# Convolution stage: the first GLU block ahead of q, its output written by parity, four weight sums in other tiles

## The chip, the cores and the metric

The kernel runs on one core of a Trainium2 chip. The metric is device time in microseconds (us): the median of the runs shown. A profiled execution gives, for every engine, when each instruction started and how long it took.

## What is computed

The reference is one layer of a streaming encoder on a sequence of 2048 tokens of 1024 channels, in fp32:

```python
h = rms_norm(x, norm_g) * (1.0 + scale) + shift          # scale, shift, gate: from silu(c) @ w_ada
u = h @ w_in                                             # 1024 -> 5632 columns
glu_in, gate_a, q, k, v, gate_b, m_a, m_b = split(u)
a, b = split(glu_in);  g = a * sigmoid(b)                # GLU, 512 channels
y_a = conv31_depthwise_causal(g) -> layer_norm -> silu, * silu(gate_a) -> @ w_conv_out
y_b = (stick_breaking_attention(rms(q), rms(k), v) * silu(gate_b)) @ w_sb_out
y = sigmoid(m_a) * y_a + sigmoid(m_b) * y_b
x = x + gate * (y @ w_out)
```

## The kernel before

Every fp32 operand of a large product is split into a rounded part `hi` and a rest `lo` (fp32r), and three matmuls (`mm3`, L135) make one product. Channels lie on the 128 partitions, tokens in four chunks of 512. The planner of the framework orders each engine's instructions by priority and by the times it expects; on each engine, and on SyncE's queue (SP) that issues the DMAs, they then run in that order. `tc.keep_in_program_order` pins some of them to program order; `pin[0]` switches this on for all matmuls, transposes and convolution taps that follow.

**Norm stage (L452 to L618).** The chunks are normed in the order of `ORDER` (3, 2, 1, 0) into the tiles `hT(g)`. The first chunk's q, k and v blocks are made here; the weights of the first q group, `w2_q0`, lie in the two pairs `whi`/`wlo` of pool `wpa` and stay there. The last chunk is normed from pool `hz` (L616): `xt` tiles are loaded, scaled, transposed by TensorE (`pt`), and `hf` minus `hhi` gives `hlo` on GpSimd (POOL) and VectorE (DVE).

**Convolution stage (L625 to L763), pool `cvp`.** It works through a fixed list of blocks (L740 to L760): q group 0 on the three later chunks, GLU 0, a SiLU gate, GLU 1, q group 1, a gate, GLU 2, k group 2, v group 4, GLU 3, k group 3, then four SiLU gates. A GLU block (`glu`, L693) is eight tiles of 24 matmuls of 512 columns: four tiles of b, whose sigmoid ScalarE (ACT) writes into `u` (L705), and four of a, which DVE multiplies into `u` (L713). `u` holds even and odd tokens in two rows. A q or k group (`qk_group`, L312) has two half tiles of 48 matmuls of 256 columns a chunk; some steps later `head_norm` (DVE) and transposes (TensorE) follow. A SiLU gate (`silu_block`, L718) has four tiles; each goes through one buffer `sg`: sigmoid on ACT, product on DVE (L726), DMA out, and only then the next sigmoid.

**Taps.** The depthwise convolution of a GLU block (`conv`, L636) is 51 DVE instructions in the list `todo`: `pre` (tile `v`), 47 taps (L661, L664) into tiles `ca`, `cc`, `cb`, and three that combine them. After each tile `tick` takes RATE of them on average from the list; what is left at the stage's end is issued there.

**Weights.** A piece (`piece`, `split_into` L98) is two halves of 512 columns: DMA into `wl` (two buffers in all), cast on ACT to `whi` (L102), rest on POOL to `wlo` (L103). The pairs rotate: two in `wpa`, one in `wpb`. Between pieces `prepare` (L220) makes two of 28 sums of blocks of w_out (for a fast product at the end of the kernel): one or two loads into `wl`, an add on POOL (L234), a cast (L237), a rest (L238), and two DMAs to DRAM (`ws_d`). A sum's rounded half goes to one tile, its rest to the other, and both lie in the rotating pairs.

After the stage come LayerNorm with the last v group and gates (L767 on), the attention with the remaining gates (L918 on), and the output products.

Of the kernel before, what the change touches and what calls it, by code (L numbers as in the profile page):

```python
# [8 lines left out]
F32 = mybir.dt.float32  # L9
F32R = mybir.dt.float32r  # L10
BF16 = mybir.dt.bfloat16
I32 = mybir.dt.int32
AF = mybir.ActivationFunctionType
ALU = mybir.AluOpType
# [4 lines left out]
P = 128  # L19
SEQ = 2048  # L20
D = 1024
KC = D // P
CH = 512
# [8 lines left out]
MAGIC = 0x5F3759DF  # L32
NXT = 6
NWA = 4
RATE = 2.9
NEARLY = 3
HT = SEQ // 2
UW = HT + CW // 2 + 1
# [3 lines left out]
B_GLU_A, B_GLU_B, B_GA = 0, 4, 8  # L42
# [3 lines left out]
def f(ap):  # L46
    return ap.bitcast(F32)
# [3 lines left out]
def trunk_kernel(  # L51
# [20 lines left out]
    nc = tc.nc  # L72
# [4 lines left out]
    def dram(name, shape, dt):  # L77
        return dp.tile(shape, dt, name=name, tag=name)
# [33 lines left out]
    pin = [False]  # L112
# [50 lines left out]
    ws_d = {}  # L163
    o_d = [[dram(f"o{j}_{g}", [P, CH], F32) for g in range(NCH)] for j in range(JC)]

    wpa = ctx.enter_context(tc.tile_pool(name="wpa", bufs=2))
# [8 lines left out]
    def hT(g):  # L175
# [7 lines left out]
    SEVEN = {  # L183
# [7 lines left out]
    }  # L191
    LASTS = {(1, 0): 4, (1, 1): 3, (0, 0): 5, (0, 1): 5}
    H = KC // 2
# [7 lines left out]
    ORDER = list(reversed(range(NCH)))  # L201
    for g in ORDER[:3]:
        h_tiles(hp, g)
    with ExitStack() as s1:
# [9 lines left out]
        def piece(src):  # L214
            npiece[0] += 1
            return load_piece(wpb if npiece[0] % 3 == 0 else wpa, src)

        wanted = [(m, j) for m in SEVEN for j in range(H)]

        def prepare():  # L220

            npiece[0] += 1
            pool = wpb if npiece[0] % 3 == 0 else wpa
            hi = pool.tile([P, 1024], F32R, tag="whi", name="whi")
            lo = pool.tile([P, 1024], F32R, tag="wlo", name="wlo")
            for i in range(2):
                m, j = wanted.pop(0)
                s = slice(i * CH, (i + 1) * CH)
                w = []
                for r, c_, _ in SEVEN[m][0]:  # L230
                    w.append(wpa.tile([P, CH], F32, tag="wl", name="wl", bufs=2))
                    nc.sync.dma_start(w[-1], w_out[j + H * r][:, c_ * CH:(c_ + 1) * CH])
                if len(w) == 2:
                    nc.gpsimd.tensor_tensor(  # L234
                        out=w[0], in0=w[0], in1=w[1],
                        op=ALU.add if SEVEN[m][0][1][2] > 0 else ALU.subtract)
                nc.scalar.copy(out=hi[:, s], in_=w[0])  # L237
                nc.gpsimd.tensor_tensor(out=lo[:, s], in0=w[0], in1=f(hi[:, s]),  # L238
                                        op=ALU.subtract)
                ws_d[m, j] = dram(f"ws{m}_{j}", [P, 2, CH], F32)  # L240
                nc.sync.dma_start(ws_d[m, j][:, 0, :], f(hi[:, s]))
                nc.sync.dma_start(ws_d[m, j][:, 1, :], f(lo[:, s]))


        def nat_mm(ps, w2, b, half, i, kc, start, stop, part=(0, 2, 1)):
# [49 lines left out]
        def tick():  # L295
# [3 lines left out]
            for d in [d for d in deferred if d[0] <= 0]:  # L299
                deferred.remove(d)  # L300
                d[1]()
            credit[0] = min(credit[0] + RATE, 3 * RATE)
            n = int(credit[0])
# [8 lines left out]
        def qk_group(grp, isk, chunks, w2=None):  # L312

            w2 = w2 or [piece(w_qkv[grp, i]) for i in range(2)]
            h4 = (grp % 2) * 4
            dst = kst_d if isk else qst_d
            for b in chunks:
                ssq = sm.tile([P, 4, 4], F32, tag="ssq", name="ssq")
                qn = qp.tile([P, 4, 4, HD], F32, tag="qn", name="qn", bufs=2)
                pss = []  # L320
                for half in range(2):
                    ps = nat_tile(pd, w2, b, half)
                    pss.append(ps)
                    for i in range(2):
                        for h in range(4):
                            sq = qp.tile([P, HD], F32, tag="sqq", name="sqq", bufs=2)
                            nc.scalar.activation(
                                out=sq, in_=ps[:, i, h * HD:(h + 1) * HD], func=AF.Square,
                                accum_out=ssq[:, 2 * half + i, h:h + 1])
                    tick()  # L330
                later(1, lambda pss=pss, ssq=ssq, qn=qn: head_norm(pss, ssq, qn))
                for pr in range(2):
                    later(3 + pr, lambda qn=qn, b=b, pr=pr: transposed(qn, pr, dst, h4, b, isk))
# [118 lines left out]
        with tc.tile_pool(name="hx", reuse_waits="tile", bufs=1) as hx:  # L452
# [33 lines left out]
            def rest(w, p):  # L486
                for i in range(2):
# [4 lines left out]
            w2_q0 = [[wpa.tile([P, D], F32R, tag=t, name=t) for t in ("whi", "wlo")]  # L492
                     for _ in range(2)]
# [6 lines left out]
            ca = hx.tile([P, D], F32, name="ca", bufs=1)  # L500
# [5 lines left out]
            for i in range(2):  # L506
                s = slice(i * CH, (i + 1) * CH)
                ps = pt.tile([P, CH], F32, tag="pt", name="pc")
# [32 lines left out]
            for kc in range(KC):  # L541
                col = slice(kc, kc + 1)
                if kc == 0:
# [4 lines left out]
                               func=AF.Identity, scale=ng[:, col], bias=ba1[:, col])  # L548
# [3 lines left out]
                hi, lo = (h[kc] for h in hT(g0))  # L552
# [72 lines left out]
        with tc.tile_pool(name="cvp", reuse_waits="tile", bufs=2, side="right") as cvp:  # L625
            ca = cvp.tile([P, D], F32, tag="cc", name="ca", bufs=1)
# [66 lines left out]
            def glu(j):  # L693
                u = cvp.tile([P, 2, UW], F32, tag="u", name="u", bufs=2)
                nc.gpsimd.memset(u[:, :, HT:], 0.0)

                def at_(g):
                    return u[:, :, g * CH // 2:(g + 1) * CH // 2].rearrange("p t m -> p m t")

                w = piece(w_in[B_GLU_B + j])  # L700
                prepare()
                for g in ORDER:
                    ps = pd.tile([P, CH], F32, tag="pd", name="pd")
                    dense(ps, w, hT(g), KC)
                    nc.scalar.activation(out=at_(g), in_=ps.rearrange("p (m t) -> p m t", t=2),  # L705
                                         func=AF.Sigmoid)
                    tick()
                w = piece(w_in[B_GLU_A + j])
                prepare()
                for g in ORDER:  # L710
                    ps = pd.tile([P, CH], F32, tag="pd", name="pd")
                    dense(ps, w, hT(g), KC)
                    nc.vector.tensor_tensor(out=at_(g), in0=ps.rearrange("p (m t) -> p m t", t=2),  # L713
                                            in1=at_(g), op=ALU.mult)
                    tick()
                conv(j, u)

            def silu_block(blk, dst, after=None):  # L718
                w = piece(w_in[blk])
                prepare()  # L720
                for g in range(NCH):
                    ps = pd.tile([P, CH], F32, tag="pd", name="pd")
                    dense(ps, w, hT(g), KC)
                    sg = cvp.tile([P, CH], F32, tag="sg", name="sg", bufs=1)
                    nc.scalar.activation(out=sg, in_=ps, func=AF.Sigmoid)
                    nc.vector.tensor_tensor(out=sg, in0=ps, in1=sg, op=ALU.mult)  # L726
                    nc.sync.dma_start(dst[g], sg)
                    tick()
# [8 lines left out]
                                half)  # L737
                        tick()

            qk_group(0, False, ORDER[1:], w2_q0)  # L740
            pin[0] = True
            for kc in range(KC):
                todo.append(lambda kc=kc: mod_col(
                    16 + kc, ca, qp.tile([P, D], F32, tag="qn", name="wa", bufs=2)))
            todo.append(lambda: nc.vector.tensor_tensor(
                out=gate, in0=mod[:, 16:24], in1=ba[:, 16:24], op=ALU.add))
            glu(0)
            silu_block(B_GA, ga_d[0])
            glu(1)
            qk_group(1, False, ORDER[1:])  # L750
# [168 lines left out]
    with ExitStack() as s2:  # L919
# [206 lines left out]
        def operands(m, ch):  # L1126

            q = "zo"[turn[0] % 2]
            turn[0] += 1
            A, B = [], []  # L1130
            for j in range(H):
                A.append(operand(q, "a", j))
                nc.sync.dma_start(f(A[j]), ws_d[m, j])
            for kc in range(H):
                B.append(operand(q, "b", kc))
                t = combined(SEVEN[m][1], lambda t: y[ch + t[1], kc + H * t[0]],
                             lambda: yp.tile([P, CH], F32, tag="io", name="sum", bufs=8),
                             nc.gpsimd)
                nc.scalar.copy(out=B[kc][:, 0, :], in_=t)
                nc.vector.tensor_tensor(out=B[kc][:, 1, :], in0=t, in1=f(B[kc][:, 0, :]),  # L1140
                                        op=ALU.subtract)
            return A, B
# [45 lines left out]
        for n_, u in enumerate(units + [None]):  # L1188
            r = [None] * 4
            p = prev[0] if prev else None  # L1190
# [67 lines left out]
    with s3:  # L1258
# [12 lines left out]
        for ch in (0, 2):  # L1271
# [6 lines left out]
            for i, m in enumerate(order):  # L1278
                A, B = nxt
# [54 lines left out]
```

## Time and profile before

| | |
|---|---|
| median of 3 runs | 1886.64 us (1884.7 to 1890.9) |
| the profiled execution | 1885.76 us, of which 1883.9 us are the span of the instructions |
| TensorE (PE) busy | 1779.0 us, 94% |
| DVE / ACT / POOL busy | 1319.4 us, 70% / 836.2 us, 44% / 815.5 us, 43% |
| mean granted TensorE clock | 0.986 |
| HBM traffic | 139 GB/s over the span |

PE's busy share counts matmuls from start to modelled end, so a busy PE is not PE at its peak; its idle time is what is read here. "Idle before" in a row is the time an engine stood still ahead of that instruction, with the instruction or transfer that ended the wait. [...]

### The profile page before, as it was taken

What the parts mean: (1) busy time and instruction counts of PE and PEld (TensorE: products, weight loads), DVE (VectorE), ACT (ScalarE), POOL (GpSimd) and SP (SyncE); (2) the same over time, 40 slices, a digit from 0 to 9 for tenths busy, and PEclk for the clock granted to TensorE, in tenths of its full rate; (3) what the DMA queues carried; (4) which work ended last, traced back from release to release, by engine and by line L of the source; (5) the groups of instructions that cost most, each with busy time, mean ns of one, the idle gap of its engine ahead of it and who ended that gap; (6) DMA issues with size and microseconds to landing.
All of it is one profiled execution on the core that took longest, in us unless ns stands there. A gap on an engine that the chain in (4) does not pass through costs nothing.

```text
span 1883.9 us, 27529 instructions
## 1 busy us (share of the span) xinstructions
PE 1779.0 (94%) x9516; PEld 1503.8 (80%) x9516; DVE 1319.4 (70%) x1769; ACT 836.2 (44%) x1916; POOL 815.5 (43%) x987
## 2 busy tenths in 40 slices
PE   6899999999999699899999999999999989999998
PEld 5798889898898587778877787877878767887887
DVE  7645598798888654448777777777777787576475
ACT  5464223232232122237767776777777762121021
POOL 0343342331414333356666666666666662321050
PEclk9999999999999899999999999999999989999999
DMA  8553733516245543342322222222223257388365
GB/s 287 168 185 107 240 117 94 192 35 196 100 133 171 173 142 136 131 168 65 99 70 93 71 82 82 93 79 84 90 80 93 68 186 246 135 301 290 135 213 167
DMA packets 138335, 263.53 MB, mean 140 GB/s; under 512 B 17746, under 2 KB 30034, under 8 KB 138196
## 3 DMA queue, kind: packets, MB, share of 16 engines
q1 hardware_dynamic: 137044, 259.68, 41.7%
q10 hardware_dynamic: 1152, 2.10, 0.3%
q8 instruction: 75, 1.23, 0.3%
q14 instruction: 64, 0.52, 0.1%
HBM read 175.73 MB, written 85.98 MB: 139 GB/s over the span
## 4 chain that ended last, share of the span: by engine, by line
PE 54%; DVE 14%; DMA 10%; POOL 8%; issue 7%; ACT 5%; SPq 2%; DVEq 0%; ACTq 0%; POOLq 0%
PE pd L115 24%; PE p L115 8%; PE po L115 7%; PE av L115 5%; PE pT L120 5%; PE z L115 5%; POOL w L999 3%; DVE sc L992 2%; POOL wlo L103 2%; DVE cc L664 2%; DMA wl<-in_w_out_dram 1%; DVE ca L664 1%; DVE cb L664 1%; DVE tlo L1026 1%; DMA wl<-in_w_qkv_dram 1%
## 5 line engine op out<-in xcount | busy, mean ns | idle before, releaser
L999 POOL TENSOR_TENSOR w<-w,sc 128x512 f32<-128x512 f32 (+1 forms) x320 | 362.6, 1134 | 256.0 <-DVE sc L992 182.3
L115 PE MATMUL pd<-hhi,whi 128*128 128x512 f32 x1024 | 412.9, 403 | 1.0 <-ACT vsg L905 1.0
L115 PE MATMUL pd<-hhi,wlo 128*128 128x512 f32 x1024 | 402.4, 393 | 0.7 <-POOL wlo L103 0.7
L115 PE MATMUL pd<-hlo,whi 128*128 128x512 f32 x1024 | 402.0, 393 | 0.0
L992 DVE TENSOR_TENSOR_SCAN sc<-z,sc,w 128x512 f32<-128x512 f32 x192 | 245.0, 1280 | 91.3 <-ACT z L988 83.7
L987 ACT ACTIVATE w<-z 128x512 f32<-128x512 f32 (+1 forms) x320 | 172.2, 538 | 129.5 <-PE z L115 104.6
L115 PEld LDWEIGHTS pd<-hhi,wlo 128*128 128x128 f32 x1024 | 193.1, 189 | 43.7 <-POOL wlo L103 1.7
L115 PEld LDWEIGHTS pd<-hhi,whi 128*128 128x128 f32 x1024 | 195.2, 191 | 35.3 <-ACT vsg L905 1.4
L115 PEld LDWEIGHTS pd<-hlo,whi 128*128 128x128 f32 x1024 | 194.0, 189 | 34.3
L1026 DVE TENSOR_TENSOR tlo<-pT,thi 128x512 fp32r<-128x512 f32 (+1 forms) x320 | 184.4, 598 | 36.5 <-ACT thi L1025 33.6
L103 POOL TENSOR_TENSOR wlo<-wl,whi 128x512 fp32r<-128x512 f32 x88 | 137.4, 1572 | 150.5 <-ACT whi L102 138.4
L115 PE MATMUL z<-kt,q 128*128 128x512 f32 (+2 forms) x640 | 193.9, 384 | 8.9 <-DVE sc L992 8.0
L1025 ACT CAST thi<-pT 128x512 fp32r<-128x512 f32 (+1 forms) x320 | 165.3, 527 | 63.0 <-PE pT L120 59.4
L115 PE MATMUL pd<-whi,hhi 128*128 128x256 f32 x608 | 171.5, 290 | 17.7 <-DVE sg L726 15.8
L120 PE MATMUL pT<-ident,w 128*128 128x128 f32 x1088 | 173.5, 275 | 8.9 <-POOL w L999 8.6
L120 PEld LDWEIGHTS pT<-ident,w 128*128 128x128 f32 x1088 | 137.9, 141 | 44.8 <-POOL w L999 13.5
L988 ACT ACTIVATE z<-z 128x512 f32<-128x512 f32 (+1 forms) x320 | 171.7, 537 | 0.0
L115 PE MATMUL pd<-whi,hlo 128*128 128x256 f32 x608 | 168.7, 287 | 1.6 <-DVE hlo L131 1.0
L115 PE MATMUL pd<-wlo,hhi 128*128 128x256 f32 x608 | 156.1, 287 | 3.4 <-POOL wlo L103 3.4
L996 DVE TENSOR_TENSOR_SCAN sc<-z,tri 128x512 f32<-128x512 f32 (+3 forms) x128 | 104.4, 820 | 52.9 <-ACT z L988 42.4
L115 PE MATMUL av<-tlo,vt 128*128 128x512 f32 (+1 forms) x320 | 123.1, 385 | 14.7 <-DVE tlo L1026 11.2
L115 PEld LDWEIGHTS pd<-whi,hhi 128*128 128x128 f32 x608 | 118.9, 196 | 18.5 <-DVE sg L726 16.2
(296 smaller groups left out, 3186.2 us busy)
## 6 DMA issues: line engine op xcount, KB each, us to landing
wl<-in_w_in_dram SPq DMA_DIRECT2D x64, 256.0 KB, 3.0
za<-ws SPq DMA_DIRECT2D x28, 512.0 KB, 4.6
oa<-ws SPq DMA_DIRECT2D x28, 512.0 KB, 4.8
wa<-in_w_ada_dram SPq DMA_DIRECT2D x24, 512.0 KB, 5.4
wl<-in_w_out_dram SPq DMA_DIRECT2D x48, 256.0 KB, 2.9
wl<-in_w_qkv_dram SPq DMA_DIRECT2D x36, 256.0 KB, 2.7
xt<-in_x_n_dram SPq DMA_DIRECT2D x16, 512.0 KB, 5.3
vst<-st SPq DMA_DIRECT2D x64, 128.0 KB, 1.9
```

The source lines that it names most:

```text
L103: (lo_eng or nc.gpsimd).tensor_tensor(out=lo[:, s], in0=wl, in1=f(hi[:, s]), op=ALU.subtract)
L115: i = nc.tensor.matmul(*a, **k)
L120: i = nc.tensor.transpose(*a)
L664: keep(nc.vector.scalar_tensor_tensor(out=acc[f_], in0=x, scalar=tap_w(f_, a), in1=acc[f_], op0=ALU.mult, op1=ALU.add))
L987: nc.scalar.activation(out=w[:, lo:], in_=z[:, lo:], func=AF.Sigmoid, scale=HD ** -0.5)
L988: nc.scalar.activation(out=z[:, lo:], in_=z[:, lo:], func=AF.Sigmoid, scale=-HD ** -0.5)
L992: nc.vector.tensor_tensor_scan(out=s[:, 1:], data0=z, data1=w, initial=s[:, 0:1], op0=ALU.mult, op1=ALU.bypass)
L996: nc.vector.tensor_tensor_scan(out=s[:, lo + 1:], data0=z[:, lo:], data1=tri[:, :CH - lo], initial=1.0, op0=ALU.mult, op1=ALU.max)
L999: nc.gpsimd.tensor_tensor(out=w[:, lo:], in0=w[:, lo:], in1=s[:, lo:CH], op=ALU.mult)
L1025: nc.scalar.copy(out=thi[:, :n], in_=pT[:, :n])
L1026: nc.vector.tensor_tensor(out=tlo[:, :n], in0=pT[:, :n], in1=f(thi[:, :n]), op=ALU.subtract)
```

## The change

RATE goes from 2.9 to 2.75. `glu(0)` is traced ahead of the first q group, and the switch `pin[0] = True` moves behind it. The q group no longer uses the weights that lie in `wpa` but loads them again. In the first GLU block the weights of a are loaded right behind those of b. `prepare` makes one sum in one tile (rounded half left, rest right) and writes it with one DMA; the four sums of the first GLU block are made in the tiles `v` and `ca` of the convolution, the others, two at a time, in a pair as before. The two GLU instructions read PSUM with a step of two elements and write each row of `u` as one contiguous piece; before, they read PSUM in order and wrote alternately to the two rows.

```diff
-RATE = 2.9
+RATE = 2.75
...
-        def prepare():
+        def prepare(t):
+            m, j = wanted.pop(0)
+            w = []
+            for r, c_, _ in SEVEN[m][0]:
+                w.append(wpa.tile([P, CH], F32, tag="wl", name="wl", bufs=2))
+                nc.sync.dma_start(w[-1], w_out[j + H * r][:, c_ * CH:(c_ + 1) * CH])
+            if len(w) == 2:
+                nc.gpsimd.tensor_tensor(
+                    out=w[0], in0=w[0], in1=w[1],
+                    op=ALU.add if SEVEN[m][0][1][2] > 0 else ALU.subtract)
+            nc.scalar.copy(out=t[:, :CH], in_=w[0])
+            nc.gpsimd.tensor_tensor(out=t[:, CH:D], in0=w[0], in1=f(t[:, :CH]),
+                                    op=ALU.subtract)
+            ws_d[m, j] = dram(f"ws{m}_{j}", [P, D], F32)
+            nc.sync.dma_start(ws_d[m, j], f(t[:, :D]))
+        def prepare_two(early=False):
+            if early:
+                for tag, n in (("v", UW), ("ca", HT + 1)):
+                    prepare(cvp.tile([P, n], F32R, tag=tag, name=tag, bufs=1))
+                return
             npiece[0] += 1
             pool = wpb if npiece[0] % 3 == 0 else wpa
...
+            for t in [pool.tile([P, D], F32R, tag=t, name=t) for t in ("whi", "wlo")]:
+                prepare(t)
...
                 def at_(g):
-                    return u[:, :, g * CH // 2:(g + 1) * CH // 2].rearrange("p t m -> p m t")
+                    return u[:, :, g * CH // 2:(g + 1) * CH // 2]
+                def by_parity(ps):
+                    return ps.rearrange("p (m t) -> p t m", t=2)
                 w = piece(w_in[B_GLU_B + j])
-                prepare()
+                wa_ = piece(w_in[B_GLU_A + j]) if j == 0 else None
+                prepare_two(j == 0)
...
-                    nc.scalar.activation(out=at_(g), in_=ps.rearrange("p (m t) -> p m t", t=2),
-                                         func=AF.Sigmoid)
+                    nc.scalar.activation(out=at_(g), in_=by_parity(ps), func=AF.Sigmoid)
...
-                w = piece(w_in[B_GLU_A + j])
-                prepare()
+                w = wa_ or piece(w_in[B_GLU_A + j])
+                prepare_two(j == 0)
...
-                    nc.vector.tensor_tensor(out=at_(g), in0=ps.rearrange("p (m t) -> p m t", t=2),
-                                            in1=at_(g), op=ALU.mult)
+                    nc.vector.tensor_tensor(out=at_(g), in0=by_parity(ps), in1=at_(g),
+                                            op=ALU.mult)
...
-            qk_group(0, False, ORDER[1:], w2_q0)
-            pin[0] = True
             for kc in range(KC):
                 todo.append(lambda kc=kc: mod_col(
                     16 + kc, ca, qp.tile([P, D], F32, tag="qn", name="wa", bufs=2)))
             todo.append(lambda: nc.vector.tensor_tensor(
                 out=gate, in0=mod[:, 16:24], in1=ba[:, 16:24], op=ALU.add))
             glu(0)
+            pin[0] = True
+            qk_group(0, False, ORDER[1:])
             silu_block(B_GA, ga_d[0])
```

## Rows read from the trace of the kernel before

**Rows 1.** Stretches: length, busy us of PE, PEld, DVE, ACT, POOL, PEclk, DMA.

```profile
125.00:168.00 43.00, 40.66 (x332) 39.53 (x332) 23.42 (x58) 26.54 (x120) 14.19 (x13) 1.00 0.34 105
168.00:213.80 45.80, 45.08 (x207) 36.67 (x205) 16.14 (x29) 11.76 (x20) 14.72 (x13) 1.00 0.73 239
213.80:420.00 206.20, 203.28 (x1181) 180.16 (x1182) 178.94 (x183) 56.53 (x233) 70.20 (x44) 1.00 0.37 121
420.00:440.00 20.00, 15.17 (x108) 14.45 (x107) 15.32 (x34) 4.85 (x21) 5.90 (x4) 0.83 0.55 179
440.00:632.00 192.00, 192.00 (x1091) 168.91 (x1089) 165.12 (x167) 46.65 (x153) 57.05 (x34) 1.00 0.45 140
632.00:655.00 23.00, 7.24 (x49) 7.19 (x49) 10.89 (x10) 5.28 (x9) 10.40 (x8) 0.70 0.62 212
```

**Rows 2.** PE's waits from 100 to 700 us: total, times, longest.

```profile
PE pd L115 <- DVE sg L726: 15.8, 1, 15.8
PE pt L120 <- DVE qn L342: 4.4, 1, 4.4
```

**Rows 3.** Timelines (start, length) and SP's waits around the first GLU block's weights.

```profile
115.84 0.88 SPq L101 DMA_DIRECT2D wl<-in_w_in_dram  x2
...
131.17 1.84 SPq L403 DMA_DIRECT2D xt<-in_x_n_dram  x4
...
165.01 1.14 ACT L102 CAST whi<-wl 128x512 fp32r<-128x512 f32 x2 [2.46 <-PE pd L115]
...
SPq L627 <- PE pt L120: 18.7, 1, 18.7
...
147.92 7.97 POOL L447 TENSOR_TENSOR hlo<-hf,hhi 128x512 fp32r<-128x512 f32 x6 [16.35 <-DVE hf L445]
...
171.81 1.29 POOL L234 TENSOR_TENSOR wl<-wl 128x512 f32<-128x512 f32 x1 [3.57 <-DMA wl<-in_w_out_dram]
...
179.98 1.30 POOL L234 TENSOR_TENSOR wl<-wl 128x512 f32<-128x512 f32 x1 [4.86 <-DMA wl<-in_w_out_dram]
...
186.19 1.07 SPq L101 DMA_DIRECT2D wl<-in_w_in_dram  x2
...
189.90 2.53 POOL L103 TENSOR_TENSOR wlo<-wl,whi 128x512 fp32r<-128x512 f32 x2 [6.59 <-ACT whi L102]
```

**Rows 4.** Chain that ended last: start, length, what; two runs of tiles.

```profile
213.77 65.14 PE pd L115 x286
...
667.20 17.27 PE pd L115 x144
```

**Rows 5.** Groups of DVE by line: busy us, mean ns, idle before.

```profile
L664 DVE SCALAR_TENSOR_TENSOR cc<-v,wsum,cc 128x1024 f32<-128x1024 f32 x56 | 92.2, 1647 | 0.0
L664 DVE SCALAR_TENSOR_TENSOR ca<-u,wdw,ca 128x1025 f32<-128x1025 f32 x60 | 87.8, 1464 | 0.0
L664 DVE SCALAR_TENSOR_TENSOR cb<-u,wdw,cb 128x1024 f32<-128x1024 f32 x56 | 86.9, 1552 | 0.0
L713 DVE TENSOR_TENSOR u<-pd,u 128x512 f32<-128x512 f32 x16 | 17.5, 1093 | 7.5 <-PE pd L115 7.4
L726 DVE TENSOR_TENSOR sg<-pd,sg 128x512 f32<-128x512 f32 x24 | 16.4, 685 | 22.0 <-ACT sg L725 21.8
...
L866 DVE TENSOR_TENSOR lsg<-gt,cv 128x512 f32<-128x512 f32 x16 | 15.3, 957 | 36.9 <-DMA gt<-ga 28.8 <-POOL cv L864 6.0 <-issue 2.2
```

**Rows 6.** Around k group 2: DVE's timeline, and one stretch as in rows 1.

```profile
420.05 2.19 DVE L670 SCALAR_TENSOR_TENSOR cc<-cc,bdw,cb 128x1024 f32<-128x1024 f32 x1
...
430.00:435.00 5.00, 3.80 (x17) 3.49 (x18) 2.39 (x6) 2.25 (x4) 1.04 (x1) 0.50 0.88 263
```

**Rows 7.** The stage's end: ACT's timeline, then the chain.

```profile
638.31 0.60 ACT L725 ACTIVATE sg<-pd 128x512 f32<-128x512 f32 x1 [1.67 <-DMA gb<-sg]
...
640.54 2.28 DVE cc L674
...
647.07 0.70 DVE sg L726
```

More of the change, by code (lines that the diff above doesn't have):

```diff
@@ L222, in prepare @@
+        def prepare_two(early=False):
[3 more added lines that the diff above has]
+                return
             npiece[0] += 1
             pool = wpb if npiece[0] % 3 == 0 else wpa
[L224 to L242, printed above, removed]
@@ L719, in silu_block @@
                 w = piece(w_in[blk])
-                prepare()
+                prepare_two()
                 for g in range(NCH):
@@ L1132, in operands @@
                 A.append(operand(q, "a", j))
-                nc.sync.dma_start(f(A[j]), ws_d[m, j])
+                nc.sync.dma_start(f(A[j]).rearrange("p s n -> p (s n)"), ws_d[m, j])
             for kc in range(H):
```

## The prediction

> **What bounds the kernel now.** I read the page's busy shares first: PE is busy 94% of the span, so a change pays only where PE stands still, or where it makes PE stand still. Then PE's idle time by stretches. From 125 us, where the first q group starts, to 213.8, where the first gate starts, PE is idle 43.00 - 40.66 + 45.80 - 45.08 = 3.1 us; from there to 420 us 2.9 us; around k group 2 20.00 - 15.17 = 4.8 us; from 440 to 632 us nothing; at the stage's end it stands still for 15.8 us [rows 1, 2]. Then what ends the two long waits. Both end on DVE: at 430 us on `head_norm`'s product, which stands in DVE's queue behind the taps, at 632 us on the last product of the gates [rows 2]. So the stage holds some 26 us that PE could win, 20.6 of them behind DVE. The change also touches the start, where there is little to win and much to lose.
>
> **Lengths that I use.** A tile of 512 columns takes 65.14 / 12 = 5.43 us (286 matmuls of 12 tiles of 24; two records are missing), a half tile of 48 narrow matmuls 17.27 / 3 = 5.76 us [rows 4]. GLU 0 is thus 8 x 5.43 = 43.4 us of PE, q group 0 6 x 5.76 = 34.5 us. Together 77.9; with 3.1 idle, the other 7.8 of the 88.8 us from 125 to 213.8 are transposes. No PE work goes or comes with the change, only its order.
>
> **1. The start: the q group's weights.** Before, GLU 0's weights were loaded at 115.84 us, but cast only at 165.01, when PE had released the pair that q held [rows 3]. PE did not miss them, since q needed no new weights. After, both pairs are free early, the b and a weights can be made ready while the first chunks are normed, and PE can run GLU on three chunks. But q's two pieces (four loads of 256 KB, four casts, four rests, all new) now stand behind six users of the two `wl` buffers: b, a and four sums. The first sum is cast into `v`, a tile of `cvp`, and this pool lies where the norm stage's pools were: SP's load of c into another `cvp` tile waited 18.7 us for the last transposes [rows 3]. I take it that `v` and `ca` lie on the `hf` tiles of the last chunk (by order of first use they come late in the pool, as `hf` does in its own). Those are read until the last `hlo` at 147.92 + 7.97 = 155.9 us [rows 3], or some 2.4 us earlier, as ACT and DVE no longer do q's squares and norms at that time. So:
> - first sum: cast at 153.5 to 155.9, its rest on POOL done 2 us later: 155.5 to 157.9;
> - three more sums: the adds of two neighbours are 179.98 - 171.81 = 8.2 us apart [rows 3]; as the next sum's first load may go ahead, 7.4 is the lower end: 177.7 to 182.5;
> - two q pieces: one took 186.19 to 189.90 + 2.53 = 192.4, so 6.2 us [rows 3]; two 12.4: 190.1 to 194.9.
>
> PE has GLU 0 done at about 125 + 43.4 + 5 (the last chunk's transposes) = 174, so it waits some 15 us. By the second piece it has done 2.2 us of q; 32.3 remain, with 2.5 of transposes: q ends at 224.9 to 229.7, where before 213.8 stood. That is 11.1 to 15.9 us lost. Behind a pause of 4.8 us the granted clock stood at 0.50, the lower level, for 3.80 busy us [rows 6], half of it lost: 1.9. Ends **11 to 18, taken +13.5** (nearer the lower end, since both ACT and DVE are freer then).
>
> What covers this cost is nothing: behind `pin`, PE may not run the gate ahead of q. The `ws` DMA that is now one instead of two hides behind the next loads, as before. The mod columns' loads of 0.5 MB still run beside the sums, as they did when the 8.2 was measured. Conv 0's `pre` and first taps wait for `v` and `ca` to be written out (some 2 us behind the last sum, 184); they and the `head_norm` behind them would wait beside PE's own wait, so I cost this at nothing; without that cover it is 2 us more.
>
> **2. Taps and GLU on DVE.** A tap takes (92.2 + 87.8 + 86.9) / 172 = 1.55 us [rows 5]. A GLU tile costs DVE 2.9 x 1.55 + 1.09 = 5.59 us against PE's 5.43: DVE falls behind in every GLU block. After: 2.75 x 1.55 + the GLU product. Written contiguously that is the gate's product of the same shape, 0.69 us [rows 5], so 4.95: DVE catches up. Bounds for the new product: 0.69 and the old 1.09 (a row that reads one operand alternately from two places took 0.96 [rows 5]); I take 0.69, since the same instruction with plain access has it. ACT's sigmoid shrinks likewise and is not on PE's path.
> As conv 0 starts six tiles earlier, the list has 78 instead of 72 tiles for its 204 items: 78 x 2.75 = 214.5. Counting through, 15, 15 and 8 items were left over at the ends of GLU 1 to 3; now 2, 3 and 0.
> - **k group 2.** The wait came with conv 1's last instructions in the middle of the group (the first at 420.05 [rows 6]). After, DVE comes in with no backlog, as before at k group 3, which had no wait (no idle time from 440 to 632 us [rows 1]). Won: 4.8 of idle and 1.9 of clock; ends 0 and 6.7, **taken -6.5**.
> - **The end.** The last but one sigmoid was done at 638.9, its product had to wait until 642.8 behind conv 3's last instruction [rows 7]: 3.9 us that go for certain, since the list now ends one tile into the last gate. The gates' products came in with a lag that grew over four blocks, part of it behind taps, part behind weight loads in SP's and ACT's queues, which stay. Product, DMA out and next sigmoid alone follow every 647.07 - 642.8 = 4.3 us, faster than PE's 5.43, so the last three tiles win back 3 us more. Ends 3.9 and 14.5 (15.8 less a sigmoid and a product), **taken -7**; late next is that lag.
>
> The 2.9 us of idle time between 213.8 and 420 us [rows 1] come from the rotation of the pairs, which is the same from the first gate on (four pairs have been used by then, as before); I let them stay.
>
> [...] The row shows that alternate writes made the product 1.09 instead of 0.69 us [rows 5]. [...]
>
> **Sum.** 13.5 - 6.5 - 7 = 0: 1885.8 us against the profiled execution, whose time lies 0.9 us below the median; taken as 1886. The forecast is that PE's idle time moves from the end to the start. Its own range is 1880 to 1893 (the bounds of the three terms, not all at one end).
>
> **Rivals.**
> - **The sums come in time (faster).** If `v` and `ca` lie on space that is free when a's weights are done, at about 131 us, four sums and two pieces end at 131 + 4 x 8.2 + 12.4 = 176, when PE comes. Then the start wins up to 2 us of the 3.1 idle: -2 - 6.5 - 7 = -15.5, **1871 us**. For it: SP issued b's loads at 115.84, long before their cast. Against it: the 18.7 us wait for `cvp`'s space [rows 3]. It decides if the first sum's cast comes before 140 us. Chance 0.30.
> - **The last chunk comes late (slower).** SP's queue is in order. If the planner puts the loads of a and of the first sum, which wait for POOL, ahead of the last chunk's `xt` loads (issued at 131.17 before [rows 3]), those wait one step of the `wl` buffers, 8.2 us, and the norm, `v`, the sums and q with them: **1894 us**. It decides if the `xt` loads start after 135 us. Chance 0.12.
> - **The parity write gains nothing.** The product stays at 1.09: DVE needs 5.35 of 5.43 us a GLU tile, catches up hardly, and keeps half of the wait at k group 2 and 2 us of the end: +5.3, **1891 us** and up to 1895. It decides above 1.0 us. Chance 0.10. [...]
>
> **Chances.** Forecast 0.43, the rivals 0.30, 0.12 and 0.10, 0.05 for what I don't see. A measurement of this kernel can tell some 0.3% (5.7 us) from no change: below 1881.0 is faster, above 1892.3 slower. Faster: 0.09 of the forecast, 0.29 of the first rival, 0.02 unseen: 0.40. Slower: 0.06 + 0.10 + 0.06 + 0.02 = 0.24. Same: 0.36. The range from 1870 to 1896 leaves out a part of the first rival and of the slow ends, together under 0.2.
>
> **What would show it.** Right, if PE is idle some 15 us ahead of q group 0 (about 175 to 190 us), ended by POOL's rest of a q piece; if the first sum's cast falls at 153 to 156 us; if there is no wait on `head_norm` at k group 2; if the wait on the last gate's product is 7 to 11 us; and if the GLU product takes 0.69 us. Wrong, if PE runs through from GLU to q, or if the gates' lag at the end vanishes or stays at 15 us.

## The result and the profile after

The changed kernel takes 1892.6 us (1886.8 to 1900.3, 20 runs) against 1885.0 us (1881.0 to 1890.9, 20 runs) for the kernel before: ratio 1.0035, 95% interval 1.0025 to 1.0045. It is slower, where no change was forecast. The profiled execution of it has a span of 1898.6 us, 14.7 more than that of before; its time, 1900.3 us, is the highest of the 20, so a second trace was taken (e1).

The same stretches as in [rows 1], of the changed kernel: start and end, length, busy time of PE, PEld, DVE, ACT, POOL, granted clock of TensorE (PEclk, a share of its full speed), share and GB/s of DMA.

```profile
125.00:168.00 43.00, 36.61 (x170) 29.00 (x169) 22.52 (x36) 19.70 (x30) 19.33 (x17) 0.96 0.51 173
168.00:213.80 45.80, 36.54 (x211) 33.27 (x211) 22.65 (x36) 9.35 (x49) 14.11 (x10) 0.81 0.48 166
213.80:420.00 206.20, 199.43 (x1123) 174.52 (x1123) 174.53 (x189) 52.96 (x229) 76.13 (x42) 0.99 0.41 127
420.00:440.00 20.00, 20.00 (x169) 20.00 (x168) 11.60 (x22) 5.30 (x48) 0.00 (x0) 1.00 0.18 67
440.00:632.00 192.00, 192.00 (x1166) 172.36 (x1165) 156.40 (x184) 49.88 (x188) 56.05 (x35) 1.00 0.45 142
632.00:655.00 23.00, 19.63 (x88) 15.84 (x86) 14.57 (x12) 4.70 (x8) 5.67 (x4) 0.99 0.54 195
```

PE's idle time has moved, as forecast: 15.7 us ahead of 213.8 us (before 3.1), none at 420 to 440. But the stretch from 213.8 to 420 us, which the prediction let stay at 2.9, holds 6.8. What PE waited for, from 125 to 213.8 us and, behind the dots, from there to 665 (total, times, longest):

```profile
PE pd L115 <- ACT whi L102: 9.3, 3, 4.3
PE pt L120 <- DVE xt L424: 5.1, 1, 5.1
...
PE pd L115 <- ACT whi L102: 6.7, 6, 2.2
PE pd L115 <- DVE sg L734: 2.6, 1, 2.6
```

The long waits of [rows 2] are gone; those on casts of weights (`whi`) are new. [rows 2] shows only the two longest: PE waited on weights before as well, on their rests, for 4.1 us in five places between 100 and 700 us:

```profile
PE pd L115 <- POOL wlo L103: 4.1, 5, 1.5
```

Of the 15.7 us ahead of 213.8, then, 9.3 are waits for q's weights; 5.1 are a wait for the last chunk, which the prediction did not have.

**The chain to q's weights.** ACT's first cast of a sum, POOL's add of the second, third and fourth sum, the rest of q's last piece, and the chain behind it (start, length):

```profile
158.52 0.62 ACT L231 CAST v<-wl 128x512 fp32r<-128x512 f32 x1 [2.65 <-DVE hlo L452]
...
164.40 1.33 POOL L228 TENSOR_TENSOR wl<-wl 128x512 f32<-128x512 f32 x1 [3.88 <-DMA wl<-in_w_out_dram]
...
173.02 1.28 POOL L228 TENSOR_TENSOR wl<-wl 128x512 f32<-128x512 f32 x1 [5.06 <-DMA wl<-in_w_out_dram]
...
180.61 1.27 POOL L228 TENSOR_TENSOR wl<-wl 128x512 f32<-128x512 f32 x1 [3.96 <-DMA wl<-in_w_out_dram]
...
194.57 1.30 POOL L103 TENSOR_TENSOR wlo<-wl,whi 128x512 fp32r<-128x512 f32 x1 [1.18 <-ACT whi L102]
...
194.54 29.80 PE pd L115 x224
```

The first cast waits for the last `hlo`, the adds are 8.6 and 7.6 us apart, q's weights are complete at 195.9 us, and only then PE runs freely.

**Marks.** To follow the time through the stage I use the ends of a few ACT instructions, read from each trace's timeline: the first sigmoid of gate 0, the first square of q group 1 and of k group 2, the first v store behind k group 2, the last sigmoid of the last gate, and the span. In us, with the ratio to the kernel before of all runs of a kernel (and its 95% interval):

| kernel | gate 0 | q 1 | k 2 | v | last gate | span | ratio |
|---|---|---|---|---|---|---|---|
| before | 219.7 | 286.6 | 391.0 | 435.2 | 647.0 | 1883.9 | 1 |
| after | 237.1 | 311.5 | 417.2 | 453.1 | 661.1 | 1898.6 | 1.0035 (1.0025–1.0045) |
| e1 after again | 234.9 | 308.3 | 412.7 | 448.6 | 656.8 | 1893.0 | 1.0064 (1.0046–1.0083) |
| e2 old order | 220.1 | 286.5 | 395.9 | 431.8 | 635.5 | 1886.4 | 0.9982 (0.9969–0.9995) |
| e3 q first | 225.4 | 294.2 | 409.8 | 445.7 | 654.4 | 1887.2 | 0.9991 (0.9975–1.0008) |
| e4 q after two sums | 221.8 | 290.6 | 394.9 | 430.8 | 639.2 | 1877.0 | 0.9959 (0.9944–0.9975) |
| e5 parity alone | 221.3 | 288.2 | 395.1 | 436.0 | 648.5 | 1887.2 | 1.0000 (0.9989–1.0011) |
| e6 old write | 235.4 | 310.9 | 417.9 | 453.8 | 663.3 | 1898.1 | 1.0066 (1.0048–1.0083) |
| e7 rests on DVE | 238.9 | 307.7 | 412.0 | 447.9 | 657.0 | 1890.7 | 1.0048 (1.0025–1.0070) |
| e8 e4 with 2.9 | 221.8 | 299.9 | 407.4 | 439.6 | 651.8 | 1887.3 | 1.0017 (1.0006–1.0027) |
| e9 e8 with e7 | 223.9 | 297.7 | 406.1 | 438.3 | 649.6 | 1881.0 | 1.0004 (0.9990–1.0019) |
| e10 e4 with e7 | 220.7 | 290.8 | 396.5 | 432.4 | 640.6 | 1875.9 | 0.9947 (0.9928–0.9966) |
| e11 2.75 alone | 223.5 | 290.5 | 399.4 | 435.3 | 643.8 | 1892.3 | 1.0027 (1.0016–1.0037) |
| e12 e4 with 2.65 | 220.5 | 289.3 | 393.6 | 429.5 | 638.4 | 1872.7 | 0.9946 (0.9932–0.9960) |

The columns are times in single traces; the ratio is what the runs of a kernel agree on. The runs were taken in four batches (after; e1 to e4; e5 to e8; e9 to e12), each with its own runs of the kernel before. The changed kernel stands in two of them, with 1.0035 and 1.0064, and the two intervals do not meet. So between batches a ratio can move by some 0.3%, more than its interval says, and smaller differences between kernels of different batches are not told apart.

### The profile page after: what moved, and what is told of

The parts are those of the page before. It is cut to its first block, busy times and chain, and to the rows that moved or that the text cites. A ratio compares the mean times of both kernels' runs of the same rounds, so it can differ in the third digit from the quotient of the medians.

```text
span 1898.6 us, 27507 instructions
## 1 busy us (share of the span) xinstructions
PE 1790.5 (94%) x9516; PEld 1511.1 (80%) x9516; DVE 1313.3 (69%) x1769; ACT 831.1 (44%) x1920; POOL 823.9 (43%) x991
## 3 DMA queue, kind: packets, MB, share of 16 engines
q8 instruction: 75, 1.23, 0.3%
## 4 chain that ended last, share of the span: by engine, by line
PE 58%; DMA 11%; DVE 10%; POOL 9%; issue 6%; ACT 4%; SPq 2%; DVEq 0%; ACTq 0%; POOLq 0%
PE pd L115 27%; PE p L115 8%; PE po L115 8%; PE av L115 5%; PE pT L120 5%; PE z L115 5%; POOL w L1007 3%; DMA wl<-in_w_out_dram 2%; POOL wlo L103 2%; DVE sc L1000 2%; DMA wl<-in_w_qkv_dram 2%; DMA wl<-in_w_in_dram 1%; POOL wl L228 1%; ACT z L996 1%; DVE tlo L1034 1%
## 5 line engine op out<-in xcount | busy, mean ns | idle before, releaser
L103 POOL TENSOR_TENSOR wlo<-wl,whi 128x512 fp32r<-128x512 f32 x92 | 147.3, 1609 | 163.5 <-ACT whi L102 159.0
L120 PEld LDWEIGHTS pT<-ident,w 128*128 128x128 f32 x1088 | 138.0, 141 | 44.8 <-POOL w L1007 13.5
L115 PE MATMUL av<-tlo,vt 128*128 128x512 f32 (+1 forms) x320 | 123.2, 385 | 17.3 <-DVE tlo L1034 14.1
```

The lines of the kernel that those rows point to most:

```text
L103: (lo_eng or nc.gpsimd).tensor_tensor(out=lo[:, s], in0=wl, in1=f(hi[:, s]), op=ALU.subtract)
L115: i = nc.tensor.matmul(*a, **k)
L120: i = nc.tensor.transpose(*a)
```

## The experiments

**e1: the changed kernel again.** No edit.

> The changed kernel once more, unchanged, for a second profile, since the profiled execution of it lay 7.7 us above its median. Theory: the start costs some 17 us in every execution (q group 0 ends at about 230 us instead of 213.8), the wait at k group 2 and about 9 us of the last gate's wait are won back, and a rest on POOL that took 10.1 us ahead of GLU 1's second half (wlo, 268 to 280 us) is an accident of that one execution. Then the time is 1890 to 1894, and in the new trace that rest takes under 3 us, with the squares of q group 1 starting at about 304 us, not 311.5. Rival: the long rest belongs to the change (DVE has no pause there); then it takes 8 to 10 us again and q group 1 starts at 311.

1896.9 us, span of the new trace 1893.0. The marks say where the 9.1 us over before lie: 15.2 at gate 0, 6.5 more from there to q group 1, nothing to k group 2, -8.3 at k group 2, -3.6 to the last gate, -0.7 behind it. The stretch from gate 0 to q 1 needs 66.9 us before; four of q group 0's six groups of transposes have moved into it, at 0.44 us each 1.8, so 68.7 would be due. The two traces of the changed kernel have 74.4 and 73.4. The rival was right: the long rest is no accident of one execution. POOL's row and DVE's rows at that place in the first trace, and the second trace's row:

```profile
268.33 11.37 POOL L103 TENSOR_TENSOR wlo<-wl,whi 128x512 fp32r<-128x512 f32 x2 [10.02 <-ACT whi L102]
...
L103 POOL TENSOR_TENSOR wlo<-wl,whi x3: 1282/2194/10127, 268.3 to 297.0; 128x512 fp32r<-128x512 f32 x3
...
267.69 1.27 DVE L669 SCALAR_TENSOR_TENSOR cb<-u,wdw,cb 128x1024 f32<-128x1024 f32 x1
268.88 1.27 DVE L669 SCALAR_TENSOR_TENSOR ca<-u,wdw,ca 128x1025 f32<-128x1025 f32 x1
...
276.06 1.27 DVE L669 SCALAR_TENSOR_TENSOR ca<-u,wdw,ca 128x1025 f32<-128x1025 f32 x1
```
```profile
265.36 11.05 POOL L103 TENSOR_TENSOR wlo<-wl,whi 128x512 fp32r<-128x512 f32 x2 [8.13 <-ACT whi L102]
```

The second row gives the shortest, median and longest rest: 1.28, 2.19 and 10.13 us. The rest that came at 268.33 us, in the middle of a tap, stood until the last of seven more taps was done at 277.3 us and ended 1.1 us later; each of these taps kept its 1.27 us. The chain through the two `wl` buffers (GLU 1's second half, two sums, q group 1's pieces) moved by that time.

**e2: the old order.** In the changed kernel, q group 0 goes first again with the weights that it had, and all sums lie in ordinary pairs.

```
+            qk_group(0, False, ORDER[1:], w2_q0)
+            pin[0] = True
             ...
             glu(0)
-            pin[0] = True
-            qk_group(0, False, ORDER[1:])
```

> The changed kernel with the old order alone: q group 0 first with the weights that it had, all sums in ordinary pairs; GLU written by parity, one sum to a tile and 2.75 taps stay. Theory: the start loses nothing (q group 0's end and GLU 0's end at about 214 us as before), the wait of 4.8 us at k group 2 is gone and the last gate's wait is some 10 us instead of 15.8, a little more than in the changed kernel since the list has six tiles less: 1885 - 7 - 5 = 1873, between 1870 and 1877. Rival: what was won behind 400 us came from conv 0 starting six tiles earlier, not from the shorter product; then DVE is late again at k group 2 and the time is 1882 to 1886.

1884.4 us: 2.2 won instead of 12. The last gate is done 11.5 us earlier than before, but nothing of it arrives. What PE waited for in the norm stage (625 to 720 us), and the chain that leads there:

```profile
PE mub L115 <- ACT hl L824: 9.0, 1, 9.0
...
649.59 1.15 DVE cc L679
650.75 2.85 DMA cv<-cc
654.37 3.14 DMA cv<-cv
```

Conv 3's last instruction is done at 650.7 us, in before at 642.8 [rows 7]: 72 tiles with 2.75 taps hold 198 of the 204 items, so conv 3 ends behind the gates and the norm stage waits for it. Between the last gate and the end this kernel needs 14.0 us more than before (1250.9 against 1236.9). Most of it lies here: where PE next waits in both traces, for `dg` of the norm stage, it does so at 690.8 us in before and at 689.6 in e2, so 1.2 us of the 11.5 are left; the rest, behind that, I have not traced. 2.75 taps need the six tiles more that GLU 0 ahead of q gives to the list.

**e3 and e4: q's pieces ahead of the sums.** The changed kernel, q group 0's weights loaded ahead of all four sums (e3) or between the second and the third (e4):

```
             w = piece(w_in[B_GLU_B + j])
             wa_ = piece(w_in[B_GLU_A + j]) if j == 0 else None
+            if j == 0:                                        # e3 here,
+                w2_q[:] = [piece(w_qkv[0, i]) for i in range(2)]
             prepare_two(j == 0)
             ...
             w = wa_ or piece(w_in[B_GLU_A + j])               # e4 behind this line
             prepare_two(j == 0)
             ...
-            qk_group(0, False, ORDER[1:])
+            qk_group(0, False, ORDER[1:], w2_q)
```

> The changed kernel with one thing moved: q group 0's two pieces of weights are loaded right behind GLU 0's, ahead of all four early sums. Theory (q waits because its pieces stand behind four sums in the chain through two buffers): q's last piece is ready by about 170 us, PE goes from GLU 0 to q without a pause, q ends at 214 to 218 us, and the time is 1892.6 - 14 = 1878, between 1874 and 1882. Rival (the loss comes from the order of the blocks itself, the transposes of the last chunk and of q, whatever the weights do): 1889 or more.

> The same with q's two pieces in the middle: two early sums ahead of them, two behind. Theory: each sum ahead costs the chain 8.2 us, so q's last piece is ready at about 180 us instead of 196, when GLU 0 is just done (182 in the trace): a wait of 0 to 4 us, time 1877 to 1883. If the first sum's wait for space (cast at 158.5) and not the number of sums sets it, little is won: 1888 or more.

e4 takes 1879.4 us, 0.41% less than the kernel before. Of e4: the rest of q's last piece, PE's waits from 120 to 235 us, and POOL's and DVE's rows at the place of the long rest of e1.

```profile
178.01 1.55 POOL L103 TENSOR_TENSOR wlo<-wl,whi 128x512 fp32r<-128x512 f32 x1 [2.77 <-ACT whi L102]
...
PE pt L120 <- DVE xt L424: 4.2, 1, 4.2
PE pd L115 <- ACT hhi L448: 0.4, 1, 0.4
PE pd L115 <- POOL u L702: 0.3, 1, 0.3
...
253.01 4.21 POOL L103 TENSOR_TENSOR wlo<-wl,whi 128x512 fp32r<-128x512 f32 x2 [7.54 <-ACT whi L102]
...
253.76 2.32 DVE L669 SCALAR_TENSOR_TENSOR ca<-u,wdw,ca 128x1025 f32<-128x1025 f32 x1
```

Two sums less ahead make q's weights complete at 179.6 us instead of 195.9: 16.3 us for two sums, 8.15 each. PE waits for no weights, and gate 0 comes 2.1 us behind before instead of 17.4. At 253 us POOL's two rests together take 4.21 us, and it is two taps, from 253.76 us on, that are stretched to 2.32 and 2.31 us; gate 0 to q 1 takes 68.8 us. So the start's loss was the chain, not the order of the blocks, and without the two losses the rest of the change is worth 7 us.

e3 takes 1884.7 us, less than in the changed kernel but not the 1878 expected. Its q pieces are complete at 165.8 us, but their rests stand on POOL between those of the last chunk, for which PE now waits (2.2 us on `hlo`), the granted clock is 0.85 from 160 to 170 us, and gate 0 is done 3.6 us behind e4. The rest, in this trace, is one POOL instruction of the kind seen in e1:

```profile
358.38 12.95 POOL L228 TENSOR_TENSOR wl<-wl 128x512 f32<-128x512 f32 x1 [9.75 <-DMA wl<-in_w_out_dram]
```

q 1 to k 2 takes 115.6 us in this trace, 104.3 in e4.

**e5, e6 and e11: what the parity write and the rate do.** e5 is the kernel before with the parity write, e6 the changed kernel with the old write (the first diff, reversed), e11 the kernel before with 2.75 taps (the second).

```
-        return u[:, :, g * CH // 2:(g + 1) * CH // 2].rearrange("p t m -> p m t")
+        return u[:, :, g * CH // 2:(g + 1) * CH // 2]
-        ps.rearrange("p (m t) -> p m t", t=2)
+        ps.rearrange("p (m t) -> p t m", t=2)
```
```
-RATE = 2.9
+RATE = 2.75
```

> The kernel before with one thing changed: sigmoid and product of GLU read PSUM by parity and write u in one piece. RATE stays 2.9, blocks and sums stay as they were. Theory: the product takes 0.69 us instead of 1.09, so a GLU tile costs DVE 2.9 x 1.55 + 0.69 = 5.19 us against PE's 5.43, DVE is not late any more at k group 2 (4.8 us of idle and its slow clock gone) and the last gate waits some 7 us less: 1886 - 8 = 1878, between 1873 and 1881. In the run with the old order and 2.75 taps (1884.4) the last gate was done 11 us earlier, but conv 3 was written out only at 654 us and the norm stage waited 9.0 us for it: there the list of taps was too long for its tiles. Rival: that loss belongs to the order of the blocks, whatever the rate; then this run gives 1883 to 1886 too, with a wait of the norm stage on conv 3.

> The changed kernel with the old GLU write (PSUM read in order, u written alternately). Theory: product 1.09 us, a GLU tile costs DVE 2.75 x 1.55 + 1.09 = 5.35 us, 0.08 below PE's 5.43: the start's loss stays, the list ends some two tiles later, and 2 to 5 us of the gains at k group 2 and the end are lost: 1895 to 1899, against 1892 to 1897 for the changed kernel. Rival: 2.75 taps and the earlier start alone keep DVE in time; then the same time as the changed kernel within 1.5 us.

> The kernel before with 2.75 taps a tile instead of 2.9 and nothing else. The run with 2.75 taps and the parity write in the old order lost its waits at k group 2 and at the last gate, but paid them back to conv 3, which was written out 11 us later (1884.4); the parity write with 2.9 taps kept the wait of 16.1 us at the last gate (1886.9). Theory: it is the rate, not the shorter product, that decides both waits: a GLU tile costs DVE 2.75 x 1.55 + 1.09 = 5.35 us, under PE's 5.43, so the wait at k group 2 is gone and the last gate waits under 5 us; conv 3 ends as late as in that run and the norm stage waits some 9 us for it: 1884 to 1888. Rival: the shorter product is needed for it; then the last gate waits 12 us or more as before, and the time is 1886 to 1890.

e5 takes 1886.9 us, the kernel before 1886.7 in the same batch: the parity write alone is worth nothing. Its product is as short as foreseen, but PE still waits 2.1 us for `head_norm` at 430 us (before 4.4), and the last gate's wait is still there. Of e5, DVE's group and PE's wait; of the changed kernel, the same group; of e6 likewise:

```profile
L716 DVE TENSOR_TENSOR u<-pd,u 128x512 f32<-128x512 f32 x16 | 10.9, 684 | 12.6 <-PE pd L115 12.5
...
PE pd L115 <- DVE sg L729: 16.1, 1, 16.1
```
```profile
L721 DVE TENSOR_TENSOR u<-pd,u 128x512 f32<-128x512 f32 x16 | 11.0, 689 | 18.9 <-PE pd L115 18.5
```
```profile
L721 DVE TENSOR_TENSOR u<-pd,u 128x512 f32<-128x512 f32 x16 | 17.5, 1092 | 17.0 <-PE pd L115 17.0
```

e6, with a product of 1.09 us, takes 1899.0 us, which its interval does not tell from the changed kernel in e1 (1.0048 to 1.0083 against 1.0046 to 1.0083; the first batch had 1.0025 to 1.0045), and from k 2 to v it needs 35.9 us, as the changed kernel does (before 44.2). e11, with the old product and the old order, needs 35.9 too, and its last gate comes 91.5 us behind the first sigmoid of the four gates (before 97.3, e5 97.6). So in the old order both waits go with the number of taps for a tile, not with the product.

They do not go with DVE's time for a tile either: 5.19 us in e5 kept them, 5.35 us in e11 did not. For k group 2 the traces show what stands in the way. In e5, as in before [rows 6], the last instructions of conv 1 stand right ahead of `head_norm` in DVE's queue; in e11 they come some 11 us behind it. Of e5 and of e11, the first of these instructions and the product of `head_norm`:

```profile
421.16 1.28 DVE L670 SCALAR_TENSOR_TENSOR cc<-cc,bdw,cb 128x1024 f32<-128x1024 f32 x1
...
431.71 1.29 DVE L342 TENSOR_TENSOR qn<-pd,qry 128x512 f32<-128x512 f32 x2
```
```profile
427.62 1.29 DVE L342 TENSOR_TENSOR qn<-pd,qry 128x512 f32<-128x512 f32 x2
...
439.52 1.27 DVE L670 SCALAR_TENSOR_TENSOR cc<-cc,bdw,cb 128x1024 f32<-128x1024 f32 x1
```

With fewer taps a tile the list runs later, and its ends meet another `head_norm`: in e11 the end of conv 0 (from 326.4 us) now stands among the instructions of q group 1's, PE waits 1.9 us there (2.5 in e2), and from q 1 to k 2 e11 needs 109.0 and e2 109.4 us, before 104.3. More than half of the 8.3 us is lost again. With GLU 0 ahead of q, conv 1 ends ahead of k group 2's first `head_norm`, with 2.75 and with 2.9 taps (in e8 at 402.8 us, the product comes at 415.1), and no trace of that order has a wait on `head_norm` of more than 0.7 us. So it is the place of the conv's end in DVE's queue that makes this wait; the rate and the six tiles more both move it. That is read from the traces; no run moves the conv's end alone.

e11 is slower all the same (1892.9 us): gate 0 and q 1 come some 4 us late, and the norm stage waits 7.9 us for conv 3:

```profile
PE mub L115 <- ACT hl L817: 7.9, 1, 7.9
```

**e7: GLU 1's rests on DVE.** In the changed kernel, `split_into(w_in[B_GLU_A + 1], hi, lo, nc.vector)` for GLU 1's second half.

> The changed kernel with the two rests of GLU 1's second piece of weights made by DVE instead of POOL. In both traces of the changed kernel the first of these rests stood on POOL for about 10 us while DVE ran some eight taps of 1.27 us without a pause, and q group 1 came 5 to 7 us later behind it than the start alone explains. [...] Rival: the chain is late anyway because q group 0's 24 stores stand ahead of the loads in SP's queue; then q group 1 still starts at 307 to 311 and the time is that of the changed kernel.

The estimate from the two traces of the changed kernel, with q group 1 some 5 us earlier, was 1889 to 1892 us. The run takes 1893.6 us, ratio 1.0048: between the two values of the changed kernel (1.0035 and 1.0064), so the runs do not show whether it is faster. The trace shows the step itself. The two rests take 0.675 us each in DVE's queue, and gate 0 to q 1 takes 68.8 us, the time that is due: the 4.6 to 5.6 us are won back there, so the stores in SP's queue, the rival, did not cause them. Shortest, median and longest of the two rests:

```profile
L103 DVE TENSOR_TENSOR wlo<-wl,whi x2: 675/675/675, 270.8 to 272.6; 128x512 fp32r<-128x512 f32 x2
```

**e8, e9 and e10: 2.9 taps in e4.** e8 is e4 with `RATE = 2.9`; e9 is e8 with e7's edit, e10 is e4 with e7's edit.

> The run with q's pieces behind two sums (1879.4), with 2.9 taps a tile instead of 2.75. Theory: with GLU 0 ahead of q the list has 78 tiles, 2.75 empties it one tile into the last gate, 2.9 some four tiles earlier, but a GLU tile then costs DVE 5.19 us instead of 4.95, still under PE's 5.43: the same time within 2 us, 1878 to 1882. Rival (DVE runs late at each rise of the rate): 1883 or more, with a wait on head_norm at k group 2.

> The run with q's pieces behind two sums and 2.9 taps (1889.0), with the two rests of GLU 1's second piece made by DVE instead of POOL. In its trace one such rest stood on POOL for 10.8 us at 256 us, behind eight taps that DVE ran without a pause, and q group 1 began 9.3 us later than with 2.75 taps, where the rest found its way after one tap. Theory: this one wait is the whole difference between 2.9 and 2.75 taps; without it the run takes 1880 to 1883. Rival (the rate itself costs the 9 us, by late products of the gates): 1887 to 1890.

> The control for the run before this: q's pieces behind two sums, 2.75 taps (1879.4, where no rest stood on POOL for over 4.3 us), with the same two rests on DVE. Theory: nothing to win here, the move of the rests alone costs or gives under 1.5 us: 1878 to 1882. Rival (rests on DVE are a gain of their own): 1876 or less.

e8 loses all that e4 had won (1889.0 us), and its trace has the loss at the same place: gate 0 to q 1 takes 78.1 us instead of 68.8. The theory for e9 fell: with the two rests on DVE the median is 1888.3 us, 0.7 less, and the ratios of the two (in two batches) have intervals that overlap. Its trace shows why moving two instructions is no cure: the next instruction on POOL, the add of a sum, takes 5.33 us there. Of e8 and of e9:

```profile
256.01 12.02 POOL L103 TENSOR_TENSOR wlo<-wl,whi 128x512 fp32r<-128x512 f32 x2 [7.12 <-ACT whi L102]
```
```profile
263.71 5.33 POOL L228 TENSOR_TENSOR wl<-wl 128x512 f32<-128x512 f32 x1 [13.81 <-DMA wl<-in_w_out_dram]
```

Gate 0 to q 1 is 73.8 us there. And 2.9 taps make the gates slower as well: from their first to their last sigmoid 96.8 and 95.8 us, against 92.9 in e4, and PE waits 6.7 and 5.7 us for the last gate's product, against 3.2 (in the old order, with 2.9 taps, it was 15.8 and 16.1). How much of e9's median is the one and how much the other is open, since its profiled execution (1882.7 us) lies 5.6 us below its median. The control e10 takes 1877.6 us (6 runs), which its interval does not tell from e4.

**e12: 2.65 taps in e4.**

> The run with q's pieces behind two sums with 2.65 taps a tile instead of 2.75. The list then holds 78 x 2.65 = 206.7 places for 204 items and ends in the last gate's third tile. Theory: the last gate's wait (3.2 us at 2.75) shrinks to under 2 us, conv 3 ends some 10 us later but still ahead of its reader: 1876 to 1880. Rival: conv 3 comes late for the norm stage, as in the old order with 2.75: 1882 or more, with a wait of the norm stage's mean on the conv's halves.

1878.8 us, ratio 0.9946: as fast as e10, and not to be told from e4 (0.9944 to 0.9975). The last gate's wait is 1.9 us, and the norm stage shows no wait on conv 3. With e4 and e10 it beats both kernels.

## Why the prediction was wrong

- **What bounds the kernel:** right. PE ran slower (granted clock 0.96 and 0.81 in the two stretches ahead of 213.8 us) or stood in just those stretches, and the loss lies ahead of the norm stage: 14.1 of the 14.7 us of the profiled execution are there at the last sigmoid; in e1 it is 9.8 us, of which 0.7 are given back.
- **The start, +13.5 (11 to 18):** the mechanism was right, term by term: four sums 8.2 us apart (8.6 and 7.6), q's weights at 190.1 to 194.9 (195.9), q's end at 224.9 to 229.7 (230.5). By the marks the loss is 17.4 and 15.2 at gate 0, with the 1.8 us of moved transposes 19.2 and 17.0 us: 3.5 to 5.7 more than taken, once above and once within the bounds. Part of it is a gain that did not come. The prediction let the last chunk come 2.4 us earlier, since ACT and DVE had less to do. Its last `hlo` was done at 159.0 us in the first trace and at 156.3 in e1, against 156.4 before. In e1 the norm did begin 2.8 us earlier, with nothing won at its end. In the first trace POOL had more to do: while it made the rests of a's weights, two of DVE's smallest steps of the norm took seven times as long, 1.23 and 1.19 us, where the same two steps right behind took 0.16 each:

```profile
141.53 0.17 DVE L89 SCALAR_TENSOR_TENSOR nx4t<-nx4y 128x4 f32<-128x4 f32 x1
141.73 1.23 DVE L91 TENSOR_TENSOR nx4t<-nx4t,ss 128x4 f32<-128x4 f32 x1
142.99 1.19 DVE L92 SCALAR_TENSOR_TENSOR nx4y<-nx4t,nx4y 128x4 f32<-128x4 f32 x1
...
141.68 2.49 POOL L103 TENSOR_TENSOR wlo<-wl,whi 128x512 fp32r<-128x512 f32 x2 [10.10 <-ACT whi L102]
```

  These two steps cost 2.1 us, and PE stood 5.1 us for the scaled chunk (3.8 in e1, 1.7 before), since the three chunks of GLU's first half were used up at 140 us, where q had filled the time before; the granted clock from 140 to 150 us was 0.83 instead of 1.00.
- **"I let them stay":** this is the step that failed. The prediction looked at the pairs' rotation between 213.8 and 420 us and not at what stands beside the rests of the weights. There one rest on POOL stood for 10.13 us behind DVE's taps, which cost 4.7 us in e1 and 5.7 in the first trace; it did not stand in the sum at all. In the prediction's terms, the sum 13.5 + 0 - 6.5 - 7 = 0 came out in e1 as 17.0 + 4.7 - 8.3 - 3.6, with 0.7 us won behind the last gate: 9.1 us. So this step is the largest error there; two terms were mis-sized beside it, the start by 3.5 us and the end by 3.4.
- **k group 2, -6.5:** 8.3 us were won, more than the upper bound of 6.7; the other 1.6 I have not traced. The wait went, but not for the cause given, that DVE's time for a tile had to fall below PE's 5.43: e5 has 5.19 and the wait, e11 has 5.35 and not. It goes with the place of conv 1's end in DVE's queue, so it is in part luck that the gain came. The rival that put the deciding point at a product of 1.0 us was wrong as well (e6).
- **The end, -7:** 3.6 to 3.8 us by the marks, less than the 3.9 that were to "go for certain"; the gates' first to last sigmoid fell from 97.3 to 92.5 us. PE's wait for a product there is 2.6 us, not 7 to 11, but other waits have come: three on casts of the next weights, and from 650 to 660 us PE is busy for only 5.0. What keeps the gates from gaining more is open.
- **The parity write:** the product takes 0.689 us, as taken, so the rival with 1.09 us did not come: read in PSUM with a step of two elements and written in one piece, it is as fast as the gate's plain one, 0.685 us [rows 5]; with the old write it takes 1.092 us (e6). But no run shows a gain by it with 2.9 taps; with 2.75 taps in the old order, e2 against e11, it goes with 8 us, together with the undivided sums, but in runs of two batches.
- **The other rivals:** the sums did not come in time (first cast 158.5 and 155.8, not before 140), and the `xt` loads were issued at 131.19 us as before.

## What to carry to other kernels

Count for each piece of weights how many pieces stand ahead of it in the chain through its staging buffers, and put what the next block needs ahead of what is only prepared for later: here the same four sums cost 15 to 17 us or 2, by the place of two pieces among them. Do not infer a wait from an engine's mean time for a tile: look which instructions stand ahead of the one that is waited for (e5, e11). A change of several parts is to be judged as a whole: 2.75 taps alone lost 0.27%, the parity write alone won nothing, the change as it stands lost 0.35%, and with two pieces moved it won 0.4%. A gain at one stage's end is none until its other inputs come as early (e2: 11.5 us earlier, 2.2 us won).

## What the runs showed of the hardware

Where a POOL instruction came during a run of DVE's taps, one or the other took longer. The median tap of a trace takes 1.28 us, the shortest POOL instruction on 128x512 1.26 to 1.29. Counted over the fourteen traces, from 200 to 665 us: 457 POOL instructions came during a tap that had another tap right behind it. 117 of them had at least five taps behind it. In 111 of these the running tap or one of the next two was stretched to 2.3 us. The other six, one in each of six traces (after, e1, e3, e5, e6, e8), were held: the POOL instruction stood for some 10 to 13 us behind seven to nine taps of 1.27 or 1.28 us, and in all six it ended 1.1 us behind the last of them. None of the 451 that were not held stood behind more than three taps; the longest of them took 5.33 us (e9). What decides between the six and the 111 is open.
